# Where 40 weight tiles of a two-layer diffusion backbone are summed: in the first output projection, or as halves in a four-tile ring of ScalarE

## The chip, the cores and the metric

One core of a Trainium2 chip runs the whole program as one launch. Its engines run side by side, each through its own queue in order: TensorE (PE) multiplies matrices, ScalarE (ACT) applies functions and copies, VectorE (DVE) does element-wise work, GpSimd (POOL) does a little of it and issues DMAs, SyncE (SP) only issues DMAs. ACT can issue DMAs as well. An instruction at the head of a queue that waits for a semaphore holds everything behind it on that engine. The metric is the device time of one execution in microseconds (us); the time before is the median of three runs.

## The reference, cut to what matters

The reference runs two layers on 1024 latent tokens and 256 context tokens of width 1024. Layer 0 mixes by a Fourier half and a Hyena half between an input and an output projection, layer 1 by neighbourhood attention. Each ends with a SwiGLU feed-forward network of inner width 2816.

```python
def reference(...):
    for i in range(DEPTH):                      # 2 layers
        ...
        y_lat = mixer_ab(u_lat, *ab)            # i = 0: ends with  concat([y_f, y_h]) @ w_out
        ...                                     # i = 1: q, k, v = split(u @ w_qkv); attention; @ w_out
        h_lat = h_lat + g1 * y_lat
        h_lat = h_lat + g2 * swiglu(modulate(rms_norm(h_lat, norm2_g[i]), sh2, sc2), w_gate, w_up, w_down)
        ...                                     # the same for the context tokens in layer 0

def swiglu(u, w_gate, w_up, w_down):
    return (jax.nn.silu(u @ w_gate) * (u @ w_up)) @ w_down
```

The sums that this case is about are not in the reference. The kernel multiplies many matrices as pairs of half-precision numbers (a high part and the rest), and scales each weight by a bound first so that the halves keep their precision. The bound of a weight tile is the sum of its absolute values.

## The kernel before

The program goes through these stages in order: filters and the input projection, the Hyena and Fourier mixers, the first output projection (`out_proj` with `w_out`), the context tokens' gate and up products of layer 0, the latents' gate and up products of layer 0 (a Winograd scheme of seven products for each pair of 256 channels, `wino_steps`), the down product, the values of layer 1 with the halves of its weights made ahead, attention, the second output projection and the feed-forward network of layer 1.

The code writes instructions in program order, and a scheduler then moves them on each engine by its own estimates of when their inputs are ready. Tiles come from pools of fixed size: 20 tiles of 128x1024 (`S4`, named s4 or s), 34 tiles of 128x512 (`S2`, named s2 or s), two each of `wh`, `wl` and `ws`. A tile is handed out again when its last reader is done, so a pool limits how far a load can run ahead.

In `out_proj`, 16 steps each load a weight tile (SP), cast it to its high part `wh` (ACT, L287), subtract for the rest `wl` (DVE, L289), and multiply (PE, L283): eight steps for the context tokens and the first 512 latent tokens, then eight for the other 512. Each step ends with an addition into the residual (DVE, L1197) and its square (ACT, L496; summed by DVE, L501), from which the norm of the next stage comes: a matmul with ones into a PSUM tile pq, a square root (ACT, L514), a broadcast (ACT, L525; PE; ACT, L529).

`qkv_sums` is the generator that `out_proj` steps once per step. It loads 44 tiles of 512 KB on POOL's queue into S4 tiles and sums each on ACT (`abs_sums`, L1251). The first four are the first gate and up blocks of layer 0, which the latents' pass needs at its start. The other 40 are the values, queries, keys and output projection of layer 1 (32 tiles) and its first eight gate and up tiles; they are used by `qkv_scales`, at the end of the latents' gate and up pass, and by `first_scales(1)` behind the down product.

In the context tokens' stage (`ffn`, the loop over 22 blocks) each block loads a gate and an up tile on SP, casts (L287) and subtracts (L289) both, multiplies (24 matmuls each) and ends with a silu (ACT, L1529) and a product (DVE, L1530). Three pairs of high and low parts are in flight. Beside it `wino_second` prepares the latents' operands (DVE L1352, L1358; ACT L1345).

Of the kernel before, what the change touches and what calls it, by code (L numbers as in the profile page):

```python
# [14 lines left out]
AF = mybir.ActivationFunctionType  # L15
# [14 lines left out]
WID = {0: 512, 1: 512, 2: 256, 3: 256, 4: 256}  # L30
OFF = {0: 0, 1: 512, 3: 512, 4: 768}
KSTART = (0, 8, 24, 32)
PAD_C, PAD_T, SHIFT = 176, 160, 16
BOPS = ("B11", "B21", "T2", "T1", "T3", "B22", "T4")


# [165 lines left out]
class Builder:  # L202
# [1050 lines left out]
    def qkv_sums(self):  # L1253

        a = self.a
        self.qs = self.C(44)
        src = [a["wv"][ch, kp] for ch in range(2) for kp in range(4)]
        src += [a[n][b] for n in ("wq", "wk", "w_out2") for b in range(KB)]
        for l, i in ((0, 0), (1, 0), (1, 1)):
            src += [a[n][l, 2 * i + k] for n in ("gate", "up") for k in (0, 1)]  # L1260
        for j, k in enumerate((32, 33, 34, 35, *range(32), *range(36, 44))):
            t = self.S4()
            self.ldr(t, src[k])
            self.abs_sums([t], self.qs[:, k:k + 1])
            if j % 3 == 2:
                yield
        yield

    def first_scales(self, l):

        keys = [(l, i, m) for i in range(l + 1) for m in (0, 1)]
        n, k = len(keys), 3 * len(self.wsc)
        q = self.qs[:, 32 + 4 * l:36 + 8 * l]
        s, inv = self.scale_cols(q, self.wcol, k, n)
        for j, key in enumerate(keys):
            self.wsc[key] = (s[:, j:j + 1], inv[:, j:j + 1])

    def qkv_scales(self):

        nc = self.nc  # L1280
        bounds = self.over_partitions(self.qs[:, :32].rearrange("p (i k) -> p i k", k=1))
        t = self.C(8)
        nc.vector.tensor_reduce(t[:, :4], bounds.rearrange("p (i k) -> p i k", k=8), axis=AX, op=MAX)
        nc.vector.tensor_scalar(t[:, :4], t[:, :4], 1e-30, None, op0=MAX)
        nc.vector.reciprocal(t[:, 4:8], t[:, :4])
        self.u1col, usi = self.operand_scale(1, 0, (0, 1))
        c = self.C(3)
        nc.vector.tensor_scalar(c[:, 2:3], t[:, 1:2], usi, 0.125, op0=MUL, op1=MUL)
        nc.vector.tensor_scalar(c[:, 0:1], c[:, 2:3], t[:, 2:3], usi, op0=MUL, op1=MUL)
        nc.vector.tensor_scalar(c[:, 1:2], t[:, 0:1], t[:, 3:4], usi, op0=MUL, op1=MUL)  # L1290
        self.wscale = {n: t[:, 4 + j:5 + j] for j, n in enumerate(("wv", "wq", "wk", "w_out2"))}
        self.qinv, self.oinv = c[:, 0:1], c[:, 1:2]
# [198 lines left out]
    def ffn(self, l, u, h, hs, second, after, keep=None, begun={}):  # L1491

        nc, a = self.nc, self.a
# [6 lines left out]
        def sums(i):  # L1500

            w = a["down"][l]
            t = [self.S2() for _ in range(4)]
            a21, a22, a11, a12 = t
            with self.follow(self.last_ld):
                for x, (k, r) in zip(t, ((0, 1), (1, 1), (0, 0), (1, 0))):
                    self.ld(x, w[2 * i + k, r])
            if i < nh:
                self.abs_sums(t, sums_of[:, 4 * i:4 * i + 4])
            nc.vector.tensor_tensor(a22, a21, a22, ADD)  # L1510
            nc.vector.tensor_tensor(a21, a11, a21, SUB)
            nc.vector.tensor_tensor(a11, a22, a11, SUB)
            nc.vector.tensor_tensor(a12, a12, a11, SUB)
            for k, x in (("S1", a22), ("S2", a11), ("S3", a21), ("S4", a12)):
                self.ldr(sops[i][k], x)
# [4 lines left out]
        if u is not None:  # L1520
            for fb in range(NFB):
# [6 lines left out]
                t = self.T()  # L1528
# [10 lines left out]
        def finish(i, gate):  # L1539

            up = self.res
            inv = self.wsc[(l, i, 1)][1]
            for k, g in gate.items():
                nc.vector.scalar_tensor_tensor(g, up[k], inv, g, op0=MUL, op1=MUL)
            if i < nh:
                self.abs_sums(list(gate.values()), sums_of[:, 4 * (nh + i):4 * (nh + i) + 4])
            b11, b12, b21, b22 = gate[(0, 1)], gate[(0, 0)], gate[(1, 1)], gate[(1, 0)]
            t1, t2, t4 = up[(0, 0)], up[(0, 1)], up[(1, 1)]
            nc.vector.tensor_tensor(t1, b12, b11, SUB)
            nc.vector.tensor_tensor(t2, b22, t1, SUB)  # L1550
            nc.vector.tensor_tensor(t4, b21, t2, SUB)
            nc.vector.tensor_tensor(b12, b22, b12, SUB)
            for k, t in zip(BOPS, (b11, b21, t2, t1, b12, b22, t4)):
                self.ldr(bops[i][k], t)

        prev = None
        waiting = {}

        def fetch(i, m):
            b = begun.get((i, m))  # L1560
            if i < n2 and (b is None or not b.whole):
                g = self.weights_ahead((l, i, m), b.w) if b else self.wino_weights((l, i, m))
                next(g)
                waiting[(i, m)] = g

        fetch(0, 0)
        for i in range(n2):
            g, up = begun.get((i, 0)), begun.get((i, 1))
            if g is None or not g.whole:
                wg = waiting.pop((i, 0))  # L1570
                w = next(wg)
                next(wg)
            fetch(i, 1)
            if g is None:
                g = Steps(self.wino_steps(w, self.G))
                g.to(1)
            if prev is not None:
                prev[0].to(7)
                finish(i - 1, prev[1])
            wu = waiting.pop((i, 1))  # L1580
            w = next(wu)
            if up is None:
                up = Steps(self.wino_steps(w, self.TK))
            if i == 0:
                for k, _ in enumerate(second):
                    if k == 11:
                        next(wu)
            next(wu, None)
            fetch(i + 1, 0)
            for k in (3, 4, 5) if i == 0 and l == 1 else ():  # L1590
                g.to(k)
                up.to(k)
            g.to(5)
            up.to(1)
            if i == n2 - 1:
                scales = self.down_scales(l, nh)
                if l == 0:
                    self.qkv_scales()
            g.to(7)
            gate = dict(self.res)  # L1600
            inv = self.wsc[(l, i, 0)][1]
            for k in ((0, 0), (1, 1), (0, 1)):
                nc.scalar.activation(gate[k], gate[k], AF.Silu, scale=inv)
            t = self.G()
            nc.scalar.activation(t, gate[(1, 0)], AF.Silu, scale=inv)
            gate[(1, 0)] = t
            up.to(5)
            prev = (up, gate)
            for k in (2 * i - 2, 2 * i - 1) if l == 1 else (9, 10) if i == 9 else (i,) if i < 9 else ():
                if 0 <= k < n2:  # L1610
                    sums(k)
            for _ in range(2):
                next(todo, None)
# [898 lines left out]
```

## Time and profile before

| what | us |
|---|---|
| median of 3 runs | 2922.55 (2908.83 to 2926.7) |
| the profiled execution, whole | 2919.95 |
| its span | 2918.2 |
| first output projection, by its last matmul | until about 845.8 |
| context tokens' gate and up products | 851.5 to 981.1 |
| latents' gate and up products of layer 0 begin | 981.1 |

The span is what the profiler saw from the first to the last instruction, and 1.75 us of the execution lie around it. Rows of the timeline give a start, a duration, the engine and line, the tiles written and read, and in brackets how long the engine had been idle and what ended that. Rows of the windows give, for each stretch of the span, how long each engine was busy in it, TensorE's granted clock (1.00 is full speed), the DMA engines' busy share and the bytes moved per second.

### The profile page before, as it was taken

Reading aid. Unit: us, or ns where it says so; the run is one execution under the profiler, and the core shown is the slowest. Engines: PE = TensorE matmul, PEld = TensorE weight load, DVE = VectorE, ACT = ScalarE, POOL = GpSimd, SP = SyncE. Lnnn points to the kernel's source line nnn. Section 1 sums busy time; section 2 is a strip of 40 time slices with the busy share of each in tenths; the row PEclk is TensorE's granted clock in tenths of the full one; section 3 lists DMA queues with packets and bytes.
Section 4 is the critical chain, followed back from the end, with each engine's and each line's share of the span. In section 5 each row is a group of like instructions: output and inputs, shape, how many; then the busy total and the mean of one; then the engine's idle time right before and its main releaser. Section 6 shows DMA issues by size and latency. Waiting matters only on the chain. (4 is left out here: it accounts for less than half of the span.)

```text
span 2918.2 us, 46050 instructions
## 1 busy us (share of the span) xinstructions
PE 2766.6 (95%) x16163; PEld 1714.2 (59%) x16163; DVE 2094.0 (72%) x3833; ACT 1647.7 (56%) x2899; POOL 642.6 (22%) x1057
## 2 busy tenths in 40 slices
PE   6989999999989999999999999999999999999998
PEld 3766557888879644444555844676665444444554
DVE  4778867585467798877886767776676778775765
ACT  4674324454675667654555555676664477654553
POOL 1012013354220121213120012444443022112000
PEclk8989999999999999999999999999999999999999
DMA  6574434358785555566994798777775666424753
GB/s 254 187 265 161 161 122 151 111 168 286 285 344 182 207 205 197 201 213 240 327 333 161 273 337 294 179 188 172 185 198 188 236 226 231 153 93 184 242 191 113
DMA packets 325156, 615.98 MB, mean 211 GB/s; under 512 B 90934, under 2 KB 130552, under 8 KB 324922
## 3 DMA queue, kind: packets, MB, share of 16 engines
q1 hardware_dynamic: 252378, 384.38, 39.9%
q0 software_dynamic: 70240, 224.45, 21.6%
q10 hardware_dynamic: 2304, 4.20, 0.4%
q8 instruction: 127, 2.08, 0.3%
q14 instruction: 107, 0.88, 0.1%
HBM read 455.33 MB, written 135.53 MB: 202 GB/s over the span
## 5 line engine op out<-in xcount | busy, mean ns | idle before, releaser
L1449 PE MATMUL ps<-s,s 128*128 128x512 f16 x2592 | 582.2, 382 | 14.4 <-ACT tk L1454 6.8
L1449 PEld LDWEIGHTS <-s 128*128 128x128 f16 x2640 | 259.0, 98 | 332.6 <-issue 27.8
L283 PE MATMUL ps<-s,wh 128*128 128x256 f32 (+3 forms) x1752 | 398.2, 331 | 11.1 <-ACT wh L287 5.4
L1218 ACT ACTIVATE s<-s,c 128x512 f16<-128x512 f32 (+1 forms) x324 | 233.5, 754 | 141.9 <-DMA s<-d 79.9
L1219 DVE SCALAR_TENSOR_TENSOR s<-s,c,s 128x512 f16<-128x512 f32 (+1 forms) x324 | 247.4, 794 | 84.5 <-ACT s L1218 84.1
L1666 PE MATMUL ps<-s 128*128 128x512 f16 (+2 forms) x1308 | 303.4, 378 | 2.0 <-DVE s L1219 2.0
L283 PE MATMUL pq<-s,wh 128*128 128x512 f16 (+1 forms) x1000 | 280.3, 354 | 9.8 <-DMA wh<-d 5.4
L283 PE MATMUL ps<-s,wl 128*128 128x256 f32 (+3 forms) x876 | 261.6, 331 | 1.3 <-DVE wl L289 1.2
L283 PEld LDWEIGHTS <-wh 128*128 128x128 f16 x1664 | 160.9, 99 | 170.2 <-issue 20.9
L1666 PEld LDWEIGHTS <-s 128*128 128x128 f16 x1536 | 148.5, 98 | 178.9 <-issue 6.5
L274 POOL DMA_DIRECT2D d<-s x201 | 109.0, 543 | 640.5 <-DVE s L1510 178.6
L283 PE MATMUL ps<-s,s 128*128 128x65 f16 (+5 forms) x2666 | 222.3, 236 | 27.5 <-DMA s<-s 11.4
L335 ACT CAST mat<-cs 128x1024 fp32r<-128x1024 f16 (+2 forms) x120 | 111.6, 935 | 140.6 <-PE ps L283 57.3
L283 PEld LDWEIGHTS ps<-s,wh 128*128 128x128 f32 x1088 | 177.5, 192 | 18.1 <-ACT wh L287 5.7
L283 PE MATMUL ps<-s,mat 128*128 128x512 f32 x696 | 184.7, 413 | 3.3 <-DVE s L289 2.9
L1449 PE MATMUL ps<-s,wh 128*128 128x512 f16 x616 | 184.9, 379 | 1.8 <-DVE g L1463 1.4
L283 PE MATMUL pq<-s,wl 128*128 128x512 f16 (+1 forms) x500 | 174.5, 354 | 0.5 <-DMA wl<-d 0.5
L283 PEld LDWEIGHTS <-s 128*128 128x128 f16 x2400 | 114.5, 98 | 82.9 <-DMA s<-s 11.5
L283 PEld LDWEIGHTS ps<-s,mat 128*128 128x128 f32 x696 | 136.5, 199 | 37.9 <-DVE s L289 3.8
L1251 ACT ACTIVATE t<-s 128x1024 bf16<-128x1024 f32 (+1 forms) x164 | 141.9, 867 | 12.2 <-DVE c L470 8.4
L283 PEld LDWEIGHTS ps<-s,s 128*128 128x128 f32 (+1 forms) x746 | 113.6, 192 | 32.1 <-ACT s L287 7.0
L283 PEld LDWEIGHTS <-wl 128*128 128x128 f16 x832 | 82.3, 99 | 77.4 <-issue 4.5
(431 smaller groups left out, 5477.3 us busy)
## 6 DMA issues: line engine op xcount, KB each, us to landing
s<-d SPq DMA_DIRECT2D x294, 256.0 KB, 4.0
d<-s POOLq DMA_DIRECT2D x157, 256.0 KB, 3.2
s<-in_down SPq DMA_DIRECT2D x154, 256.0 KB, 5.4
s<-in_ada_w POOLq DMA_DIRECT2D x48, 512.0 KB, 4.8
g<-in_bias POOLq DMA_DIRECT2D x128, 192.0 KB, 3.6
s<-in_gate SPq DMA_DIRECT2D x46, 512.0 KB, 3.7
s<-in_up SPq DMA_DIRECT2D x46, 512.0 KB, 4.0
d<-g POOLq DMA_DIRECT2D x87, 256.0 KB, 2.9
```

The source lines that it names most:

```text
L274: self.last_ldr = self.nc.gpsimd.dma_start(out, in_).ins
L283: self.nc.tensor.matmul(o, l, r, start=st, stop=sp)
L335: self.nc.scalar.copy(m, st)
L1218: nc.scalar.activation(hi, src, AF.Copy, scale=scale)
L1219: nc.vector.scalar_tensor_tensor(lo, src, scale, hi, op0=MUL, op1=SUB)
L1251: self.nc.scalar.activation(junk[:, :t.shape[1]], t, AF.Abs, scale=2.0 ** -15, accum_out=st[:, k:k + 1])
L1449: nc.tensor.matmul(ps, x[:, sl], y, start=first and j == 0 and x is wh and y is xh, stop=j == 3 and x is wl, skip_group_check=True)
L1666: m = nc.tensor.matmul(acc[j][:, c0:c1], x[:, sl], y[:, xs], start=first and k == 0, stop=last and k == 2, skip_group_check=True)
```

## The change

Of the 44 sums only the first four stay in the output projection. The other 40 tiles are summed as 80 halves of 128x512 by a new generator `later_sums`, which `ffn` creates in layer 0 and steps by two at four places of each of its 11 blocks, and drains before `qkv_scales`. It takes four S2 tiles as a ring and issues the loads on ACT's own queue: four loads first, then for each half a sum in place (with its accumulated output to a column of `qs`), followed by the load of the half that is four further. The columns grow from 44 to 84, and a padding tile shrinks by as much.

```diff
-PAD_C, PAD_T, SHIFT = 176, 160, 16
+PAD_C, PAD_T, SHIFT = 136, 160, 16
...
     def qkv_sums(self):
 
         a = self.a
-        self.qs = self.C(44)
+        self.fs = self.C(4)
+        for j in range(4):
+            t = self.S4()
+            self.ldr(t, a[("gate", "up")[j // 2]][0, j % 2])
+            self.abs_sums([t], self.fs[:, j:j + 1])
+        yield
+
+    def later_sums(self):
+
+        a, nc = self.a, self.nc
+        self.qs = self.C(80)
         src = [a["wv"][ch, kp] for ch in range(2) for kp in range(4)]
         src += [a[n][b] for n in ("wq", "wk", "w_out2") for b in range(KB)]
-        for l, i in ((0, 0), (1, 0), (1, 1)):
-            src += [a[n][l, 2 * i + k] for n in ("gate", "up") for k in (0, 1)]
-        for j, k in enumerate((32, 33, 34, 35, *range(32), *range(36, 44))):
-            t = self.S4()
-            self.ldr(t, src[k])
-            self.abs_sums([t], self.qs[:, k:k + 1])
-            if j % 3 == 2:
-                yield
+        src += [a[n][1, 2 * i + k] for i in (0, 1) for n in ("gate", "up") for k in (0, 1)]
+        src = [x[:, c:c + 512] for x in src for c in (0, 512)]
+        ring = [self.S2() for _ in range(4)]
+        for t, x in zip(ring, src):
+            self.lda(t, x)
         yield
+        for j in range(len(src)):
+            t = ring[j % 4]
+            nc.scalar.activation(t, t, AF.Abs, scale=2.0 ** -15, accum_out=self.qs[:, j:j + 1])
+            if j + 4 < len(src):
+                self.lda(t, src[j + 4])
+            yield
...
-        q = self.qs[:, 32 + 4 * l:36 + 8 * l]
+        q = self.qs[:, 64:80] if l else self.fs
...
-        bounds = self.over_partitions(self.qs[:, :32].rearrange("p (i k) -> p i k", k=1))
+        bounds = self.over_partitions(self.qs[:, :64].rearrange("p (i k) -> p i k", k=2))
...
+        later = self.later_sums() if l == 0 else iter(())
+        next(later, None)
+
+        def some(n=2):
+            for _ in range(n):
+                next(later, None)
+
...
             fetch(i, 1)
+            some()
...
             fetch(i + 1, 0)
+            some()
...
             up.to(1)
+            some()
             if i == n2 - 1:
+                some(80)
                 scales = self.down_scales(l, nh)
...
             prev = (up, gate)
+            some()
```

The scheduler does not leave the sums where the code writes them. Of the 80 halves it places 8 ahead of the end of the output projection's last step, 66 in the context tokens' stage and 6 at the start of the latents' pass. DVE's, PE's and SP's queues keep their instructions and change places only between the output projection and the fifth block or so of the latents' pass; on POOL the 40 loads are gone. Three places show it.

The first is PE at the end of the output projection. The ps tiles with s and 128x512 are the last step, pq is the norm's sum with ones (c), the 128x256 rows are the first context weight. Before:

```order
L283 MATMUL ps_8420<-s_1586_6313,wh_8378 128x512
L283 MATMUL ps_8420<-s_1587_6314,wh_8378 128x512
L283 MATMUL ps_8420<-s_1586_6313,wl_8379 128x512
L283 MATMUL pq_8457<-c_91,tk_8140 128x1 x4
L283 MATMUL ps_8627<-s_1895_7956,wh_8616 128x256
L283 MATMUL ps_8627<-s_1896_7957,wh_8616 128x256
```

Now, at the same place of the queue:

```order
L283 MATMUL ps_8260<-s_1584_6311,wl_8227 128x512
L283 MATMUL ps_8260<-s_1586_6313,wh_8226 128x512
L283 MATMUL ps_8260<-s_1587_6314,wh_8226 128x512
L283 MATMUL ps_8260<-s_1586_6313,wl_8227 128x512
L283 MATMUL ps_8467<-s_1855_7876,wh_8456 128x256
L283 MATMUL ps_8467<-s_1856_7877,wh_8456 128x256
```

The four matmuls of the norm no longer stand between the stages; they follow inside the second context weight, which the scheduler now puts behind most of the third, some 50 matmuls later.

The second is ACT at the same moment. L496 is the square of the last step, L514 the norm's root, the casts L287 from s tiles are the context weights. Before:

```order
L496 ACTIVATE tk_8446<-s_1926_8038 128x512
L1251 ACTIVATE t_8324,c_7389<-s_1995_8322 128x1024
L514 ACTIVATE st_8462<-pq_8457,c_95 128x4
L1251 ACTIVATE t_8363,c_7389<-s_2002_8361 128x1024
L287 CAST wh_8616<-s_2304_8615 128x1024
L1251 ACTIVATE t_8367,c_7389<-s_2004_8365 128x1024
L287 CAST wh_8622<-s_2307_8621 128x1024
L287 CAST wh_8682<-s_2313_8681 128x1024
```

Now, where the ring's tiles are s_2438 to s_2441, and L1277 and L271 are a ring's sum and load (the first context weight's cast stands a little ahead of these rows):

```order
L271 DMA s_2438_9994<-in_wq 128x512
L271 DMA s_2439_9995<-in_wq 128x512
L271 DMA s_2440_9996<-in_wv 128x512
L271 DMA s_2441_9997<-in_wv 128x512
L1277 ACTIVATE s_2438_9994,c_9993<-s_2438_9994 128x512
L1277 ACTIVATE s_2439_9995,c_9993<-s_2439_9995 128x512
L287 CAST wh_8462<-s_2227_8461 128x1024
L271 DMA s_2438_9994<-in_wq 128x512
L1277 ACTIVATE s_2440_9996,c_9993<-s_2440_9996 128x512
L271 DMA s_2439_9995<-in_wq 128x512
L496 ACTIVATE tk_8286<-s_1886_7958 128x512
L1277 ACTIVATE s_2441_9997,c_9993<-s_2441_9997 128x512
```

Sums of whole tiles whose loads POOL had issued stood beside the casts before; now sums stand a few rows behind the load of the same tile, on the same queue, ahead of the next casts.

The third is ACT some 20 us on, ahead of the seventh context weight. L529 is the norm's broadcast, L1345 (now L1358) the latents' operands. Before, the seventh weight's cast is the last of these rows:

```order
L1529 ACTIVATE t_8809<-ps_8759 128x256
L529 COPY t_8465<-pq_8470 128x512
L1345 CAST s_2333_8817<-s_1931_8060 128x512
L1345 CAST s_2333_8817<-s_1934_8069 128x512
L287 CAST wh_8821<-s_2334_8820 128x1024
```

Now it stands eight rows behind the last of these (L1542 is the former L1529):

```order
L271 DMA s_2440_9996<-in_wv 128x512
L529 COPY t_8305<-pq_8310 128x512
L1277 ACTIVATE s_2440_9996,c_9993<-s_2440_9996 128x512
L271 DMA s_2441_9997<-in_wv 128x512
L271 DMA s_2438_9994<-in_wk 128x512
L271 DMA s_2439_9995<-in_wk 128x512
L1277 ACTIVATE s_2441_9997,c_9993<-s_2441_9997 128x512
L271 DMA s_2440_9996<-in_wq 128x512
L1542 ACTIVATE t_8649<-ps_8599 128x256
L271 DMA s_2441_9997<-in_wq 128x512
L1277 ACTIVATE s_2438_9994,c_9993<-s_2438_9994 128x512
L1277 ACTIVATE s_2439_9995,c_9993<-s_2439_9995 128x512
```

Between the broadcast and the operands' casts stand four sums and five loads that were not there.

## The prediction

> **What bounds the kernel now.** I read the page first, then the windows around the two stages that the change joins, then the waits of PE, then both queues' timelines where PE is not busy.
>
> ```profile
> span 2918.2 us, 46050 instructions
> PE 2766.6 (95%) x16163; PEld 1714.2 (59%) x16163; DVE 2094.0 (72%) x3833; ACT 1647.7 (56%) x2899; POOL 642.6 (22%) x1057
> core 0: us, PE busy (x) PEld busy (x) DVE busy (x) ACT busy (x) POOL busy (x), PEclk, DMA share, GB/s
> 740.00:750.00 10.00, 10.00 (x59) 8.73 (x58) 3.39 (x5) 7.68 (x15) 4.14 (x8) 1.00 1.03 416
> 750.00:760.00 10.00, 10.00 (x59) 8.73 (x58) 4.58 (x8) 6.60 (x11) 3.78 (x7) 1.00 1.03 420
> 840.00:850.00 10.00, 6.90 (x34) 5.41 (x32) 3.07 (x5) 7.65 (x16) 3.78 (x7) 0.99 1.03 420
> 850.00:860.00 10.00, 8.08 (x49) 7.79 (x50) 4.89 (x5) 6.54 (x10) 0.00 (x0) 0.67 1.03 421
> 870.00:880.00 10.00, 6.17 (x40) 5.77 (x39) 9.01 (x12) 4.67 (x7) 0.54 (x1) 0.86 0.82 311
> 876.00:980.00 104.00, 103.80 (x901) 103.80 (x902) 77.45 (x98) 56.51 (x79) 10.30 (x19) 0.98 0.55 192
> ```
>
> PE bounds the program. In the stretches of the output projection it is busy for 10.00 of 10 us, though ACT has sums there and the DMA engines are full; from 876 to 980 it is busy for 103.80 of 104. So a sum taken out of 740 to 760, or put behind 876, costs PE nothing by itself. Only around the boundary of the two stages does PE stand still, and there its waits are for ACT and DVE:
>
> ```profile
> PE ps L283 <- ACT wh L287: 5.4, 2, 3.1
> 845.44 0.40 PE L283 MATMUL ps<-s,wl 128*128 128x512 f32 x1
> 848.08 1.05 PE L283 MATMUL pq<-c,tk 128*128 128x1 f32 x8 [2.23 <-DVE tk L501]
> 851.46 0.79 PE L283 MATMUL ps<-s,wh 128*128 128x256 f32 x2 [2.33 <-ACT wh L287]
> 852.71 0.58 PE L283 MATMUL ps<-s,wl 128*128 128x256 f32 x1 [0.47 <-DVE wl L289]
> 874.94 0.50 PE L283 MATMUL ps<-s,wh 128*128 128x256 f32 x2 [3.07 <-ACT wh L287]
> 876.20 0.38 PE L283 MATMUL ps<-s,wl 128*128 128x256 f32 x1 [0.76 <-DVE wl L289]
> ```
>
> The last matmul of the output projection ends at 845.84. PE then idles 2.23 us for the norm's sum and 2.33 us for the first context weight, with a granted clock of 0.67 over the ten microseconds after; and 3.07 + 0.76 us at the seventh context weight. ACT's queue tells why:
>
> ```profile
> 842.70 1.04 ACT L1251 ACTIVATE t<-s 128x1024 bf16<-128x1024 f32 x1
> 843.74 1.04 ACT L1251 ACTIVATE t<-s 128x1024 bf16<-128x1024 f32 x1
> 846.67 0.63 ACT L496 ACTIVATE tk<-s 128x512 f32<-128x512 f32 x1 [0.76 <-DVE s L1197]
> 849.17 0.26 ACT L514 ACTIVATE st<-pq,c 128x4 f32<-128x4 f32 x1 [0.83 <-PE pq L283]
> 849.33 1.05 ACT L1251 ACTIVATE t<-s 128x1024 bf16<-128x1024 f32 x1
> 850.37 1.04 ACT L287 CAST wh<-s 128x1024 fp32r<-128x1024 f32 x1
> 864.74 1.27 ACT L525 ACTIVATE t<-c,st 128x128 f32<-128x128 f32 x4
> 866.03 1.28 ACT L1529 ACT_TABLE_LOAD   x1
> 867.32 0.66 ACT L1529 ACTIVATE t<-ps 128x256 f32<-128x256 f32 x2
> 869.72 0.59 ACT L529 COPY t<-pq 128x512 f32<-128x512 f32 x1 [0.98 <-PE pq L283]
> 872.39 0.62 ACT L1345 CAST s<-s 128x512 f16<-128x512 f32 x1 [2.09 <-DVE s L1358]
> 873.85 2.94 ACT L287 CAST wh<-s 128x1024 fp32r<-128x1024 f32 x3
> ```
>
> The first weight's cast (850.37) stands behind a sum and behind the norm's root, which waits for PE. The seventh (873.85) stands behind the norm's broadcast and the latents' operands. What is late at the seventh cast is late at the end of the stage, since PE has no slack from there on.
>
> **Removed.** 40 whole sums: they start 1.04 us apart (842.70, 843.74), so 41.6 us of ACT; and 40 loads on POOL's queue.
>
> ```profile
> L274 POOL DMA_DIRECT2D s<-in_wv x8: 530/530/530, 722.0 to 731.9; - x8
> s<-in_wv POOLq DMA_DIRECT2D x8, 512.0 KB, 13.4
> L1251 ACT ACTIVATE t<-s 128x512 bf16<-128x512 f32 x72 | 45.2, 629 | 2.4 <-DMA s<-in_down 1.7
> 1451.82 0.63 ACT L496 ACTIVATE tk<-s 128x512 f32<-128x512 f32 x1 [1.78 <-DVE s L1687]
> 1451.83 0.34 ACTq L271 DMA_DIRECT2D d<-s  x1
> ```
>
> 40 x 0.53 = 21 us of POOL, and 20 MB from DMA engines that are full there (share 1.03). PE was at 10.00 of 10 beside all of it, so the gain inside the output projection is nothing; if that cover were wrong it could be no more than the PE idle there, of which these rows show none. At the boundary the gain is real: the norm's matmuls no longer stand between the stages, and the first weight is cast ahead of the square of the last step (the queues' rows above), so 2.23 + 2.33 + 0.47 us can go, and with them part of the slow clock.
>
> **Added.** 80 sums of 0.63 us = 50.4 us on ACT, 8.8 more than before because of the fixed part of each, and 80 loads issued by ACT. The only issue by ACT that the trace has begins 0.01 us after an activation and lies beside it, so it costs 0 there and 0.34 alone; I take 0.1, nearer the first, as most loads have a sum in front of them. Where the trace is silent is the wait: a sum stands in ACT's queue a few rows behind the load of its own tile, and the load could only be issued once the previous sum of that tile was done. Behind a waiting sum are queued the casts of the context weights (PE waits), the silus and the norm's root and broadcast (DVE and PE wait).
>
> From PE's last output matmul to the seventh weight's cast, ACT's new queue holds 20 half sums (12.6 us), four casts (0.95 each by the three in 2.94: 3.8), a square, root, broadcast, table load, three silus, the copy of the broadcast and two operand casts (0.53 + 0.26 + 1.27 + 1.28 + 1.1 + 0.59 + 1.1 = 6.1): 22.5 us, and 2.0 for the 20 issues. They cannot start sooner, because two tiles of the ring are given out only when those matmuls are done. So without a wait the seventh cast comes at 845.84 + 24.5 = 870.3, 3.5 us before its time of 873.85. In this stretch there are seven separate places at which a sum follows its load with two other sums (1.3 us) between. With a landing time L each costs L - 1.3. Rows for L:
>
> ```profile
> cs<-in_vf_l SPq DMA_DIRECT2D x32, 256.0 KB, 2.7
> s<-in_gate SPq DMA_DIRECT2D x15, 512.0 KB, 3.3
> s<-in_down SPq DMA_DIRECT2D x154, 256.0 KB, 5.4
> s<-in_gate SPq DMA_DIRECT2D x9, 512.0 KB, 13.5
> ```
>
> The first is a lone load of the ring's size, the second a load of twice the size in the window 876 to 980, the third loads of this size in a bunch, the fourth the window 826 to 870, where the DMA engines are full. After the change POOL's loads are gone from there, so I take L = 3.0, between the first two: -3.5 + 7 x 1.7 = **+8.4**. By 2.7 it is +6.3, by 3.3 +10.5, by 5.4 +25.2. The Trainium skill, page "DMA: Bandwidth & Descriptors", section "Anatomy of one DMA — SWDGE (gpsimd) path", fits a transfer as about 2.0 us plus its bytes over 436 GB/s, which gives an estimate of 2.6 us for 256 KB and a term of +5.6; by that rule 512 KB take 3.2 us, and the trace's 3.3 agrees, though on another queue than the page's.
>
> Behind the seventh weight ACT has room: 56.5 busy of 104 us, plus 46 sums of 0.63 = 85.5, which leaves 18.5 us for waits before ACT and not PE sets the pace; the loads also run further ahead there. I take 0.
>
> **Moved.** Six sums reach the start of the latents' pass, two of them straight behind their loads and ahead of the copy that PE already waits for:
>
> ```profile
> 993.58 1.87 PE L1449 MATMUL ps<-s,s 128*128 128x512 f16 x4 [2.87 <-ACT g L1454]
> ```
>
> Two waits of up to 2 us there cost 0 (if the copy is held by PE anyway) to 4; I take 1.6. SP's last two weight loads of the output projection stand behind six loads of gate and up; in a stage where PE is fed ten microseconds ahead (13.4 us to land without a PE gap) this costs nothing, else a PE gap of a landing, 3 us. SP's and ACT's loads now share their completion semaphores, so either may wait for the other: 0 taken, the high end is in the second rival.
>
> **Sum.** 2919.95 (the profiled execution: span 2918.2 and 1.75 around it) + 8.4 + 1.6 = **2930**. That execution is 2.6 below the median of the runs, which lie 18 apart.
>
> **Rivals.** *The ring keeps up, and the boundary closes (faster).* If the ring's loads land within the two sums between, L at or below 1.3 at most of the seven places, or if each wait finds ACT with nothing else due, then the removed waits win: -3.5 by the queue, and up to 2.23 + 2.33 + 0.47 + 3.07 + 0.76 = 8.9 if the seventh cast too is no longer late: 2911 to 2921 with the third term at 0 to 1.6. The point from which it decides is L = 1.8, where 7 x 0.5 is the 3.5 gained. For it: the DMA engines lose 20 MB in the stage before. Against it: no load of 256 KB in the rows above lands in under 2.7 us. Chance 0.22, since some of the seven may lie where ACT waits for PE anyway.
>
> *The ring's loads land as in a bunch (much slower).* SP, with the S4 tiles that POOL's loads no longer hold, sends its gate and up loads in one go, and the ring's loads come in among them at 5.4 us or later: 25.2 + 1.6, so 2947, and up to 15 us more if some of the 46 later sums use up the 18.5 us of room: 2942 to 2962. The row of 13.5 us speaks for it, the 192 GB/s from 876 on against it. The Trainium skill, same page, section "Issuing engines are not separate DMA queues", says that transfers of all engines run on the same 16 DMA engines and interleave, so a queue of its own would not save the ring from this; no row of this trace shows loads on ACT's queue. Chance 0.15.
>
> *The sums do not go where the change says.* This is so by the rows of the queues: 66 of 80 land in the context stage. Had they stayed in the latents' pass, the term of 8.4 would be gone. It is no case of its own.
>
> **How the numbers follow.** The forecast's own range is 2922 (L = 1.9 and nothing at the pass's start) to 2940 (L = 3.9): chance 0.58. With 0.22 and 0.15 for the rivals 0.05 is left, half on each side. The range 2913 to 2950 leaves out the lowest part of the first rival (0.05), the upper part of the second (0.07) and the rest. One per cent, about what a measurement of this kernel tells from no change, is 29 us: 2893 to 2952. Slower than that: the upper 0.4 of the second rival and the rest above, 0.08; faster: 0.02; within: 0.90.
>
> **What would show it.** PE's gap at 845.8 gone or under 1 us, and the first context weight multiplied at once. Sums of the ring with idle time before them that ended with a DMA, seven or so of 1 to 2 us, between 846 and 880. The seventh weight's cast some 8 us later than 873.85, counted from the end of the output projection, and PE busy without a break from there to the end of the stage. The landing median of the loads on ACT's queue near 3 us. It is wrong if the output projection itself gets shorter or longer by more than 3 us (then PE was not the bound there), if ACT waits for the ring all through the context stage, or if loads on ACT's queue hold ACT at the issue itself.

## The result: 0.44% slower, and where it went

The change takes 2931.72 us (median of 20 runs, 2920.71 to 2940.35) against 2917.74 us before (20 runs, 2906.78 to 2927.85): a ratio of 1.0044, 95% interval 1.0031 to 1.0058, or 14.0 us. The profiled execution of the change is the fastest of its twenty. It is some 7 us ahead of the other's when the stretches compared below begin and gains another 5 behind them, so the spans of the two profiles (2918.9 and 2918.2) say little; stretches between the same matmuls say more.

The windows of the kernel after, in the columns of those before (the last two are cuts of 870 to 880):

```profile
core 0: us, PE busy (x) PEld busy (x) DVE busy (x) ACT busy (x) POOL busy (x), PEclk, DMA share, GB/s
740.00:750.00 10.00, 10.00 (x59) 8.71 (x57) 3.21 (x5) 1.94 (x3) 1.08 (x2) 1.00 0.31 109
840.00:850.00 10.00, 10.00 (x84) 9.79 (x83) 3.89 (x5) 7.04 (x17) 0.54 (x1) 1.00 0.70 220
876.00:980.00 104.00, 100.97 (x865) 99.89 (x866) 74.35 (x92) 82.87 (x169) 9.18 (x17) 0.98 0.92 331
871.00:876.00 5.00, 0.00 (x0) 0.00 (x0) 0.63 (x2) 1.92 (x5) 0.00 (x0) 0.50 0.99 355
877.00:879.00 2.00, 1.54 (x8) 1.50 (x8) 0.45 (x1) 0.93 (x3) 0.00 (x0) 0.50 0.59 207
```

In the output projection ACT falls from 7.68 to 1.94 of 10 us and the DMA share from 1.03 to 0.31, and PE has exactly the 10.00 that it had: nothing gained there. From 840 to 850 PE is now busy throughout (6.90 before): the gap between the stages is gone. But PE does nothing at all from 871 to 876. Its timeline after:

```profile
841.02 0.40 PE L283 MATMUL ps<-s,wh 128*128 128x256 f32 x2
858.06 0.80 PE L283 MATMUL ps<-s,wh 128*128 128x256 f32 x2 [2.11 <-ACT wh L287]
876.24 0.80 PE L283 MATMUL ps<-s,wh 128*128 128x256 f32 x2 [9.77 <-ACT wh L287]
877.50 0.58 PE L283 MATMUL ps<-s,wl 128*128 128x256 f32 x1 [0.46 <-DVE wl L289]
985.37 0.61 PE L1462 MATMUL ps<-s,wh 128*128 128x512 f16 x2
990.00 2.75 PE L1462 MATMUL ps<-s,s 128*128 128x512 f16 x12 [1.86 <-ACT g L1467]
995.08 4.44 PE L1462 MATMUL ps<-s,s 128*128 128x512 f16 x12 [2.33 <-ACT g L1467]
```

The first context matmul (841.02) follows the last of the output projection with no idle time, where 5.6 us lay before (845.84 to 851.46). The seventh context weight has a gap of 9.77 us, where it had 3.07. The granted clock falls within it (1.00 from 866 to 869, 0.83 from 869 to 870) and stays at 0.50 until about 880, though PE is busy again from 876.24 on. Before, the gap of 3.07 us at the seventh weight was followed by half the clock too (0.57 from 877 to 881), so the work that runs at half speed behind the gap is much the same in both, 3 to 4 us. The Trainium skill, page "TensorE: Matmul & The Clock Gate", section "What's actually happening", gives half the clock after an idle window of about 3.4 us and the full one only after as much sustained work. The trace agrees at this gap, with about 4 us of work at half the clock; it differs in that shorter gaps were enough elsewhere, the 3.07 us before and 1.69 and 2.11 us after (0.51 from 856 to 863).

What ACT did in between, first as the list of its waits from 841 to 876 (us in total, times, longest), then as the rows of its timeline that hold those waits, and the seventh weight's cast:

```profile
ACT s L1277 <- DMA s<-in_wv: 7.2, 4, 3.8
ACT s L1277 <- DMA s<-in_wq: 5.2, 3, 3.1
```

```profile
841.77 0.63 ACT L1277 ACTIVATE s<-s 128x512 f32<-128x512 f32 x1 [0.97 <-DMA s<-in_wq]
848.69 0.63 ACT L1277 ACTIVATE s<-s 128x512 f32<-128x512 f32 x1 [1.32 <-DMA s<-in_wv]
850.20 0.63 ACT L1277 ACTIVATE s<-s 128x512 f32<-128x512 f32 x1 [0.79 <-DMA s<-in_wv]
852.88 0.63 ACT L1277 ACTIVATE s<-s 128x512 f32<-128x512 f32 x1 [1.16 <-DMA s<-in_wq]
862.77 0.63 ACT L1277 ACTIVATE s<-s 128x512 f32<-128x512 f32 x1 [1.23 <-DMA s<-in_wv]
867.31 0.63 ACT L1277 ACTIVATE s<-s 128x512 f32<-128x512 f32 x1 [3.82 <-DMA s<-in_wv]
874.53 0.63 ACT L1277 ACTIVATE s<-s 128x512 f32<-128x512 f32 x1 [3.08 <-DMA s<-in_wq]
875.16 1.03 ACT L287 CAST wh<-s 128x1024 fp32r<-128x1024 f32 x1
```

Seven sums wait for their own tile's load, 12.4 us together, and the seventh weight's cast (875.16) stands behind the last of them. The same list before has 0.6 us of waits of sums for a DMA (843 to 876). How long the ring's loads take to land (826 to 985, third figure the median in us):

```profile
s<-in_wv ACTq DMA_DIRECT2D x12, 256.0 KB, 3.3
s<-in_wq ACTq DMA_DIRECT2D x16, 256.0 KB, 4.0
s<-in_wk ACTq DMA_DIRECT2D x16, 256.0 KB, 5.9
```

For the comparison of all kernels I cut PE's timeline at matmuls that all of them have, in the same order: A is from a matmul of the Fourier mixer (at 695.1 before), some 30 us ahead of the output projection's first one, to the end of the output projection, B from there to the seventh context weight, C to the first latents product, D from there 61 matmuls on, E from there to the matmul that stands at 1300.1 before. All in us of one profile each.

| kernel | ratio to before (95%) | A | B | C | D | E |
|---|---|---|---|---|---|---|
| before | 1 | 150.7 | 29.1 | 106.2 | 19.2 | 299.8 |
| the change | 1.0044 (1.0031 to 1.0058) | 153.0 | 35.2 | 109.1 | 21.4 | 299.3 |
| e1 sums, no reloads | 0.9978 (0.9966 to 0.9991) | 154.5 | 21.8 | 107.8 | 19.4 | 300.3 |
| e2 reloads, no sums | 0.9972 (0.9953 to 0.9991) | 155.1 | 18.3 | 105.1 | 19.0 | 302.0 |
| e3 neither | 0.9951 (0.9934 to 0.9969) | 151.2 | 18.3 | 104.1 | 17.7 | 302.3 |
| e4 held to the latents' pass | 1.0083 (1.0061 to 1.0105) | 153.3 | 18.3 | 104.1 | 27.4 | 332.0 |
| e9 the same, no reloads | 0.9986 (0.9971 to 1.0002) | 153.7 | 18.3 | 104.1 | 25.1 | 303.3 |
| e5 held to the tenth weight | 1.0026 (1.0011 to 1.0040) | 150.5 | 18.3 | 110.8 | 19.9 | 312.2 |
| e6 the same, ring of 12 | 1.0099 (1.0077 to 1.0121) | 155.7 | 18.3 | 138.1 | 19.2 | 299.4 |
| e7 ring loads by POOL | 1.0043 (1.0025 to 1.0061) | 156.9 | 31.5 | 107.7 | 21.2 | 300.9 |
| e8 24 whole, 16 as halves | 0.9987 (0.9972 to 1.0003) | 154.7 | 18.3 | 109.9 | 17.7 | 302.3 |
| e10 the same, paced | 0.9969 (0.9955 to 0.9984) | 152.8 | 18.3 | 104.1 | 19.4 | 300.5 |
| e11 80 halves, paced | 1.0070 (1.0046 to 1.0093) | 152.9 | 20.5 | 132.0 | 23.8 | 301.3 |
| e12 the same, loads by POOL | 1.0020 (1.0009 to 1.0031) | 151.2 | 19.1 | 112.0 | 23.3 | 301.4 |

Change against before: A +2.3, B +6.1, C +2.9, D +2.2, E -0.5, so 13.0 us, beside the 14.0 of the medians. The intervals of e8 and e9 include no change.

### The profile page after: what moved, and what is told of

Its sections match the earlier page's. It is cut to its first block, busy times and chain, and to the rows that moved or that the text cites. A ratio compares the mean times of both kernels' runs of the same rounds, so it can differ in the third digit from the quotient of the medians.

```text
span 2918.9 us, 46111 instructions
## 1 busy us (share of the span) xinstructions
PE 2756.2 (94%) x16163; PEld 1703.1 (58%) x16163; DVE 2090.3 (72%) x3833; ACT 1652.3 (57%) x2979; POOL 619.9 (21%) x1017
## 5 line engine op out<-in xcount | busy, mean ns | idle before, releaser
L283 PE MATMUL ps<-s,s 128*128 128x65 f16 (+5 forms) x2666 | 221.4, 236 | 23.3 <-DMA s<-s 7.0
L283 PEld LDWEIGHTS ps<-s,wh 128*128 128x128 f32 x1088 | 177.4, 192 | 28.8 <-ACT wh L287 16.9
L1218 ACT ACTIVATE s<-t,c 128x512 f16<-128x512 f32 x172 | 114.9, 711 | 28.5 <-DVE c L1330 17.4
```

What stands on the lines that cost most here:

```text
L283: self.nc.tensor.matmul(o, l, r, start=st, stop=sp)
L1218: nc.scalar.activation(hi, src, AF.Copy, scale=scale)
```

## The experiments

The theory W: sums that stand in ACT's queue right behind their own tile's load wait for the landing and hold the casts behind them. The rivals: A, it is ACT's added work; D, the ring's 20 MB slow the weights' loads; Q, it lies in ACT's queue of DMAs. All edits are against the changed kernel.

**The two halves of the cost apart (e1, e2, e3).** e1 takes away the reloads and with them the waits:

```diff
-        ring = [self.S2() for _ in range(4)]
+        ring = [self.S2() for _ in range(5)]
...
-            nc.scalar.activation(t, t, AF.Abs, scale=2.0 ** -15, accum_out=self.qs[:, j:j + 1])
-            if j + 4 < len(src):
-                self.lda(t, src[j + 4])
+            nc.scalar.activation(ring[4], t, AF.Abs, scale=2.0 ** -15, accum_out=self.qs[:, j:j + 1])
```

> Leaves out the 76 reloads: the ring's first four tiles are loaded once and summed over and over (into a fifth tile), so the 80 sums keep their 50 us of ScalarE work but none waits for a landing. Theory W (sums that stand in ScalarE's queue right behind their own tile's load hold the context weights' casts): the gap of TensorE ahead of the seventh context weight falls from 9.8 us to under 4, the stretch from the end of the output projection to the seventh weight from 35 to 27 us or less, and the kernel lands 5 to 12 us below the one before. Rival A (it is the 9 us more of ScalarE work, moved to where the casts are): the gap stays at 8 us or more and the kernel 8 to 14 us above the one before.

e2 takes away the sums and lets POOL issue the loads:

```diff
+        nc.vector.memset(self.qs, 1.0)
...
-            self.lda(t, x)
+            self.ldr(t, x)
...
-            nc.scalar.activation(t, t, AF.Abs, scale=2.0 ** -15, accum_out=self.qs[:, j:j + 1])
             if j + 4 < len(src):
-                self.lda(t, src[j + 4])
+                self.ldr(t, src[j + 4])
```

> Leaves out the 80 sums and lets GpSimd issue the 80 ring loads, so the 20 MB still move through the same stretch while ScalarE has neither sum nor issue (the scales are constants). Theory W: no loss at the seventh weight (gap under 4 us), the kernel 5 to 12 us below the one before. Rival D (the ring's 20 MB delay the loads of the context weights, which land in 6 us in place of 3.3): the gap stays near 10 us and the kernel 5 to 14 us above the one before.

e3 takes away both:

```diff
-        ring = [self.S2() for _ in range(4)]
-        for t, x in zip(ring, src):
-            self.lda(t, x)
+        nc.vector.memset(self.qs, 1.0)
...
-            t = ring[j % 4]
-            nc.scalar.activation(t, t, AF.Abs, scale=2.0 ** -15, accum_out=self.qs[:, j:j + 1])
-            if j + 4 < len(src):
-                self.lda(t, src[j + 4])
```

> Leaves out the 40 weight tiles altogether: neither loads nor sums (constants in their place). It gives what the removal from the output projection is worth by itself. By the trace of before: 2.2 + 2.3 + 0.5 us at the boundary and up to 3.1 + 0.8 at the seventh weight, so 5 to 12 us below the kernel before under every theory; if it is level with before, the removed part was worth nothing and the loss after is smaller than reckoned.

PE at the seventh context weight in e1:

```profile
865.80 0.51 PE L283 MATMUL ps<-s,wh 128*128 128x256 f32 x2 [2.15 <-ACT wh L287]
```

The gap is 2.15 us in place of 9.77, with all 80 sums still on ACT and in this stage, 16 of them in B (19 in the change). The kernel is 5.7 us below before, inside what W expected. In e2 and e3 PE has no gap ahead of that matmul, so 18.3 us is the floor of B: what it costs when nothing of the sums stands in ACT's queue. In e2 this holds though the ring's bytes move:

```profile
847.50:865.80 18.30, 18.30 (x156) 17.81 (x155) 11.00 (x16) 11.47 (x19) 5.92 (x11) 1.00 0.93 344
```

Of the 16.9 us that the change has over the floor, the work of the sums makes at most 3.5 (e1) and the moved bytes 0 (e2). The rest, 13.4, goes with the reloads on ACT's queue: the waits for their landings, with the half clock behind PE's gaps, and their issues, which e1 takes away as well and e7 below tries by themselves. That decides for W in B. The kernel before has 10.8 us over the floor there, which is the gain that the change reached for; e3's median is 14.6 us below before, a little over the 5 to 12 expected. e2's 6.6 us below before lie 8 above e3, 3.9 of them in A: there the bytes do cost (see "Why the prediction held").

**The sums held back (e4, e9, e5, e6).** By the words of the change the sums belong in the latents' pass. A hold on the ring's first loads puts them there, behind the last context weight's cast (fb 21):

```diff
                 lo = self.last_lo
+                if fb == 21:
+                    self.hold = self.last_hi
...
-        for t, x in zip(ring, src):
-            self.lda(t, x)
+        with self.follow(self.hold):
+            for t, x in zip(ring, src):
+                self.lda(t, x)
```

> The change with the first four ring loads queued on ScalarE behind the last cast of the context stage, so that all 80 halves fall in the latents' gate and up pass. Theory W: the casts of the context weights are free of waits (gap at the seventh weight under 4 us) and the gain of the boundary stays, so 2 to 10 us below the kernel before, less what the waits cost in the latents' pass. Rival A: ScalarE's 50 us are then missing in the latents' pass, and the kernel is as slow as the change or slower (8 to 20 us above before).

e9 is e4 with the edit of e1 (five tiles, no reloads).

> The run that held all 80 halves behind the context stage, but without the 76 reloads (the first four tiles are summed over and over), so the latents' pass has the sums' 50 us of ScalarE work and no wait for a landing. Theory W: the 39 us that the 80 sums cost from the first latents product on shrink to under 12 and the kernel is at or below the one before. Rival A: they stay at 25 us or more and the kernel is 12 us or more above before.

PE's waits for g, the copy of a product that ACT makes, from the first latents product on, in e4 and then in e9 (us in total, times, longest; the largest item in e4, the second in e9):

```profile
PE ps L1463 <- ACT g L1468: 18.3, 8, 6.3
```

```profile
PE ps L1461 <- ACT g L1466: 6.0, 2, 3.8
```

e4 came out 0.83% or 28 us above before, on rival A's side and beyond its 8 to 20, but not for A's reason: with the same sums and no reloads (e9, level with before) D and E together take 328.4 us in place of 359.4, against 320.0 without any sum (e3). The work of 80 sums costs 8 us in the latents' pass; the reloads cost 31, and the waits for them go with it: ACT's sums wait 30.2 us for loads in e4 and 2.4 in e9. The context stage itself is at its floor in both (B 18.3, C 104.1), as W said.

In e5 the hold is the tenth weight's cast (the second weight of the block fb == 4), and 37 sums are left for the latents' pass; e6 is e5 with twelve tiles:

```diff
-        ring = [self.S2() for _ in range(4)]
+        ring = [self.S2() for _ in range(12)]
...
-            t = ring[j % 4]
+            t = ring[j % 12]
...
-            if j + 4 < len(src):
-                self.lda(t, src[j + 4])
+            if j + 12 < len(src):
+                self.lda(t, src[j + 12])
```

> The change with the first four ring loads queued behind the tenth context weight's cast; 43 of 80 halves then stand ahead of the last context cast and 37 in the latents' pass. Theory W: the seventh weight comes 18.3 us after the first context matmul as in the run without sums and loads; the 37 sums in the latents' pass cost what the 80 did in the run that held all of them there, (1321.3 - 962.0) - (1280.2 - 960.2) = 39 us for 80, so 18 us, and the context stage 3: the kernel 4 to 10 us above before. A rival (only the place at the boundary was bad) has it 8 to 14 us below before.

> As the run before with twelve tiles in the ring in place of four, so that a load runs up to twelve sums ahead; all 80 halves then stand ahead of the last context cast. Theory W (waits for the landing): no sum waits long, the context stage takes 104 us plus at most 8 for ScalarE's 50 us of sums, and the kernel is 5 to 12 us below before. Rival A (ScalarE's work): it is then the bound of the context stage, 10 us or more over 104, and the kernel within 3 us of before.

e5 kept to its numbers in the whole (5.5 us above before), though C lost 6.7 us where 3 were given, and D and E 12 where 18 were. e6 missed on both sides: C is 34 us over its floor and the kernel 26 us above before, where W had 5 to 12 below and A within 3. PE and SP's queue in e6:

```profile
892.99 0.80 PE L283 MATMUL ps<-s,wh 128*128 128x256 f32 x2 [5.84 <-ACT wh L287]
```

```profile
SPq L268 <- DMA s<-in_wv: 37.5, 6, 29.1
```

Two things stand there that neither theory had. With so many tiles ready the scheduler puts eight to twelve sums (5 to 7.5 us) between two casts at six places, while PE has two weights ahead, 2 x 2.8 us by (18.3 + 104.1) / 44. And SP, which loads the context weights, waits for landings of ring loads. How the 34 us divide between the two is not shown for e6; the second is tried by itself in other kernels.

**Whose queue (e7, e8, e10, e11, e12).** e7 is the change with both `self.lda` of the ring replaced:

```diff
-            self.lda(t, x)
+            self.ldr(t, x)
...
-                self.lda(t, src[j + 4])
+                self.ldr(t, src[j + 4])
```

> The change with the ring's 80 loads issued by GpSimd in place of ScalarE; the sums and the ring are the same. Theory W: the sums still wait for the landing, a load starts no sooner, so the gap at the seventh context weight stays at 6 us or more and the kernel 5 to 16 us above before. Rival Q (ScalarE's own queue: the 80 issues and the completion semaphores that it shares with SyncE's loads): gap under 4 us, the kernel at or below before.

SP's waits from 826 to 1000 in the kernel before, in the change, and in e7:

```profile
SPq L268 <- DVE wl L289: 96.6, 34, 9.2
```

```profile
SPq L268 <- DMA s<-in_wq: 50.0, 4, 34.7
SPq L268 <- DVE wl L289: 21.7, 12, 4.7
SPq L268 <- DMA s<-in_wk: 20.2, 5, 9.4
```

```profile
SPq L268 <- DVE wl L289: 124.6, 33, 12.3
```

Before, SP waits for a weight tile to come free (DVE's last reader). In the change it waits for loads that ACT issued; in these traces the loads of SP and of ACT use the same eight completion semaphores (POOL's have eight others), and a load waits until the one ahead on its semaphore has landed. With POOL issuing, that is gone, and yet e7 is as slow as the change: B is still 31.5 (the gap at the seventh weight is split over three), because the sums wait for landings all the same, 13.5 us in six waits from 841 to 876. ACT's waits and then PE's gaps in e7:

```profile
ACT s L1277 <- DMA s<-in_wv: 7.2, 2, 5.0
ACT s L1277 <- DMA s<-in_wq: 6.3, 4, 2.2
```

```profile
849.24 0.74 PE L283 MATMUL ps<-s,wh 128*128 128x256 f32 x4 [3.83 <-ACT wh L287]
862.83 0.51 PE L283 MATMUL ps<-s,wh 128*128 128x256 f32 x2 [1.40 <-ACT wh L287]
873.90 0.79 PE L283 MATMUL ps<-s,wh 128*128 128x256 f32 x2 [2.92 <-ACT wh L287]
```

The single gap at the seventh weight, 2.9 us, is below the 6 that W expected and by itself meets Q's under 4; the sum over the stretch does not, and the kernel is 12 us above before. So Q explains nothing of the slowdown as a whole that these runs resolve (interval 0.25 to 0.61%), though 3.7 us of B may be its share. The Trainium skill, page "DMA: Bandwidth & Descriptors", section "Issuing engines are not separate DMA queues", says that another issuing engine saves no more than the issue. For e7 against the change (1.0043 and 1.0044) the runs agree; for e12 against e11, below, they do not.

e8 leaves 24 tiles whole in the output projection and holds the other 32 halves back as e5 does:

```diff
+        self.qs = self.C(80)
+        self.nc.vector.memset(self.qs, 0.0)
+        for j, x in enumerate(self.later_src()[:24]):
+            t = self.S4()
+            self.ldr(t, x)
+            self.abs_sums([t], self.qs[:, 2 * j:2 * j + 1])
...
+        src = self.later_src()[24:]
...
-            nc.scalar.activation(t, t, AF.Abs, scale=2.0 ** -15, accum_out=self.qs[:, j:j + 1])
+            nc.scalar.activation(t, t, AF.Abs, scale=2.0 ** -15, accum_out=self.qs[:, 48 + j:49 + j])
```

> 24 of the 40 tiles stay whole in the output projection (loads by GpSimd, all their sums ahead of the first context cast), the other 16 are 32 halves in the ring of four, whose first loads are queued behind the tenth context weight's cast. Theory W: nothing of the sums is left where TensorE waits for a cast, so the boundary's gain stays and the context stage loses 1 to 3 us: 8 to 14 us below before. Against it: if the 24 whole sums still crowd the boundary, the gain falls to 0 to 5 us.

e10 is e8 with the ring stepped by the context loop itself, each step queued behind that block's second cast (e11: all 80 halves, `fb >= 1`, four steps for each block, ring of eight; e12: e11 with `self.ldr`):

```diff
+                if fb >= 3:
+                    for _ in range(1 if fb == 3 else 2):
+                        with self.follow(self.last_hi):
+                            next(later, None)
```

> 24 whole tiles in the output projection as before; the 32 halves of the other 16 are paced by hand, two behind every second context cast from the tenth on, with a ring of four, so that a load has two blocks (11 us) to land. Theory W with bunches (what counts is the work and the wait that stand between two casts, against the two weights that TensorE has ahead): the context stage takes at most 2 us more than the 104.1 without sums, the kernel 8 to 14 us below before. If the sums' work as such cost it, as in the run with the same 32 halves unpaced (5.8 us more), it is 3 to 5 us below before.

> All 80 halves paced, four behind every second context cast from the sixth on, ring of eight, so a load has two blocks to land. Theory W with bunches: 2.5 us of sums between two casts are less than what TensorE has ahead, so the seventh weight comes under 20 us after the first context matmul, the context stage takes 104 to 110 us, the kernel 4 to 14 us below before. Rival A (ScalarE's work in this stage) and rival D (20 MB more in it): 110 us or more, the kernel at or above before.

> The paced run of all 80 halves with the ring's loads issued by GpSimd in place of ScalarE. That run's context stage took 132 us, with SyncE waiting 30.9 and 26.4 us for landings of ring loads and ScalarE's issues waiting for landings of SyncE's. Rival Q (SyncE's and ScalarE's loads take turns on the same completion semaphores, so each queue waits for the other's landings): SyncE no longer waits for a ring load, the stage from the seventh weight on falls to 104 to 112 us and the kernel to 2 to 14 us below before. Rivals A and D (ScalarE's 50 us of sums and the 20 MB in the stage, both unchanged): the stage stays at 120 us or more, the kernel 15 us or more above before.

SP's waits from 826 to 1000 in e8, then in e10 (the first lines of each list, which is in order of their totals):

```profile
SPq L268 <- DMA s<-in_w_out: 48.3, 6, 28.1
SPq L268 <- DVE wl L289: 33.3, 17, 4.2
```

```profile
SPq L268 <- DVE wl L289: 90.8, 33, 6.2
```

The same 32 halves with the same ring: unpaced, SP waits for ring loads and C is 5.8 us over the floor, where 1 to 3 were expected; paced, with a load two blocks ahead of its sum, the waits for in_w_out are gone (11.8 us in three waits for loads of in_gate are the largest left for a DMA) and C is at the floor to a tenth. Pacing changes two things at once, the sums between two casts and SP's waits, and these two runs don't part them. e8 is 4.3 us below before by the medians, short of the 8 to 14 expected and not clear of no change. e10 is 0.31% below before (interval 0.16 to 0.45%) and has the lowest ratio of the kernels that sum every tile; it is faster than before and than the change, while its interval overlaps that of e8. Its 5.5 us between the medians, or 9 by the ratio's point, stand at the lower end of what was expected or short of it.

e11 missed: B is near its number (20.5), but C takes 132.0 where 104 to 110 were expected. SP's waits (the first three lines) and ACT's own timeline there:

```profile
SPq L268 <- DMA s<-in_up: 42.8, 7, 10.2
SPq L268 <- DMA s<-in_wv: 30.9, 4, 29.6
SPq L268 <- DMA s<-in_wq: 26.4, 8, 11.9
```

```profile
887.06 3.44 ACTq L271 DMA_DIRECT2D s<-in_wq  x3
890.54 0.62 ACT L1371 CAST s<-s 128x512 f16<-128x512 f32 x1 [4.40 <-DMA s<-in_wq]
```

Here three issues by ACT span 3.44 us (one alone takes 0.33, the median of the sixteen in the trace of before), since the second and the third wait for earlier loads to land, and they hold the casts behind them for 4.40 us. With the loads on POOL (e12) SP waits for tiles to come free again:

```profile
SPq L268 <- DVE wl L289: 108.5, 32, 8.8
```

C falls from 132.0 to 112.0 with the same sums, the same bytes and nearly the same places. So of e11's 28 us over the floor 20 are Q: SP and ACT waiting on their shared semaphores for landings, of the other's loads and of their own. 8 are left for A and D, which these two runs don't part; e2 bounds D, since there POOL moves most of the ring's bytes in C (318 GB/s from 866 to 971, where e12 has 315 from 850 to 985) and C is 1.0 us over the floor. The kernel is still 0.20% above before, not below as expected: to the 8 come 5.6 in D, where the last sums fall.

## Why the prediction held, and where its terms were off

- **PE bounds the output projection, and the sums cost nothing there.** Right: 10.00 of 10 with and without them. Stretch A grew by 2.3 us all the same. The prediction had this as the w_out loads behind six others on SP, "costs nothing, else a PE gap of a landing, 3 us": PE has a gap of 1.98 + 0.52 us there, behind a cast that waited 3.64 us for that load. A lies between 150.5 and 156.9 over the runs, but most of that scatter is in its first part, the end of the Fourier mixer, which no edit touches (29.8 to 34.9 us). From the output projection's first matmul to its last, before takes 120.9 us and the change 122.8, so this term is 1.9 us. Its cause is not the six loads alone: in e3, e4 and e5 SP has the same six ahead, no ring load moves yet, and the stage takes 120.8 to 121.4 without a gap at that load; in e2 and e7, where POOL issues the ring's first loads, it takes 125.3 and 124.8. The ring's own first loads, beside the six, make that w_out load late (13.3 us to land in the change, 10.6 in e4).
- **The boundary's gap goes.** Right, wholly: 5.6 us to none.
- **The seventh weight is late by +8.4.** Right in kind, a little too large. From the end of the output projection (841.18) its cast comes after 34.0 us; predicted were 36.4, before it took 28.0, so the term measured 6.0. Seven waits at 1.7 us, 11.9 in all, were predicted; seven came, with 12.4 in all, but uneven, two of them 3.8 and 3.1. The queue without them took 21.6 us, not 24.5. That the waits are the cause, and not the work, is shown by e1 and e7 against the change. Of ACT's issues the prediction says that the trace has one; it has sixteen, all from s tiles to d, at 0.33 us in the median, so its 0.1 for an issue stands on one row of them.
- **The later sums cost 0.** Wrong by 2.9 us (C). The prediction counted ACT's room in the mean (18.5 us), and a mean does not hold between two casts: PE, forecast without a break from the seventh weight on, still waits 2.8 us for high and low parts (wh, wl) from 877 to 986. e1 has 107.8 without waits, so 1.6 of the 2.9 go with the sums' work alone; e8 and e10, e11 and e12 show that places and issuing queue decide how much such sums cost. The shared completion semaphores, named in the prediction and taken at 0, cost little in the change itself (e7 has 1.4 less in C, 3.7 less in B and 3.9 more in A) and 20 us in e11.
- **The start of the latents' pass, +1.6.** Measured +2.2.
- **The sum.** +10 by the terms, 13 between the profiles and 14.0 between the medians: the direction and the mechanism held, and the whole is short by the 2.3 of A, the 2.9 of C and 0.6 of D. That the term of 8.4 was 2.3 too large against B's 6.1 made up for part of this, and the forecast's start, 2919.95, lies 2.2 above the median of twenty runs; that 2930 is so near to 2931.72 is to that extent luck.
- **The range.** Its ends don't come out of the terms named for them: L = 1.9 and nothing at the pass's start give 2920.7, not 2922, and L = 3.9 with the full 4 us there 2938.7, not 2940.
- **The rivals.** The faster one did not come, because landings took 3.3 to 5.9 us (medians) and not 1.3; that its condition was the right one is shown by e1, which takes the waits away and is 0.22% faster than before. The much slower one had its landings (5.9 us at the median of the loads of in_wk), but mostly behind the seventh weight, where they cost little. "The sums do not go where the change says" was true. The prediction took it that the term of 8.4 would then be gone; had the sums gone there it would have been worse, e4, 0.83% above before, since they wait in the latents' pass as well.

## What to carry to other kernels

An instruction that waits for a load on an engine's in-order queue holds everything queued behind it until the landing, so what counts is how far in time a load is issued ahead of its use, against a landing under load (here 3.3 to 6 us), and not the number of tiles in the ring: e8 and e10 have the same 32 halves and four tiles, one 5.8 us over the floor in C and the other at it, and e6 with twelve tiles is the slowest kernel here. The Trainium skill, page "DMA: Bandwidth & Descriptors", section "Rules for kernel authors", has it as issuing early and waiting late. The trace agrees: e4 against e9, 31 us, is the price of not doing so here. Filler work on an engine that also feeds TensorE is better paced by hand, a little between any two feeds: in e6 the scheduler, with many tiles ready, put eight to twelve sums between two casts. And before an engine is chosen to issue loads, look in the trace whether another queue then waits for their landings.

## What was not expected of the chip and the program

- Two DMA queues held each other: in the change SP waited 50.0 us in four waits for loads that ACT had issued, and in e11 three issues by ACT spanned 3.44 us. Moving the same loads to POOL took 20 us off one stage (e12) and changed nothing in the time of another kernel (e7), where the sums still waited for landings.
- The ring's loads, issued by POOL and with no sums (e2), cost nothing in B and 1.0 us in C, but PE has a gap of 2.90 + 0.53 us at the end of the output projection, where one weight load landed late among them.
- Removing the sums and their loads altogether (e3) is worth 0.49%, more than the waits listed at the boundary. The seventh weight's gap and the half clock behind it go as well: B falls from 29.1 to 18.3 and C from 106.2 to 104.1.
